# Low weight parts by accumulating DMA onto minus the high part, and small copies moved to ScalarE

## The chip, the cores and the metric

The kernel runs on one core of a Trainium2 chip. The core has five engines with a queue each: TensorE (PE in the profile; PEld is its weight load), VectorE (DVE), ScalarE (ACT), GpSimd (POOL) and SyncE (SP), which here only issues transfers. 16 DMA engines move data between DRAM and the on-chip memory (SBUF); TensorE writes to PSUM. The metric is the device time of one execution in microseconds (us): 1533.71 us, the median of three runs (1533.48 to 1533.86).

## The reference

Two layers of an encoder are applied to 640 tokens: 512 of a prompt, and 8 running streams of 16. In float32:

```python
# layer 0: mixer A|B, then ConvFFN; layer 1: attention with forget gates, then ConvFFN
def _conv_ffn(x, prev, w_up, conv_w, w_down):
    z, st = _causal_dwconv(x @ w_up, conv_w, prev)   # width 3; st: the last two rows of x @ w_up
    gate, up = jnp.split(z, 2, axis=-1)
    return (jax.nn.silu(gate) * up) @ w_down, st

hp = _rmsnorm(xp, norm_ffn[layer])                   # d_model 1024, d_ff 2816
yp, st_p = _conv_ffn(hp, zero_f, w_up[layer], conv_ffn[layer], w_down[layer])
xp = xp + yp
```

The streams start the convolution from saved rows, and `st` (two rows for each stream and for the prompt) is an output. The ConvFFN is the "channel mixer" of this text; there are two of them.

## The kernel before, in words

Activations lie with features on the 128 partitions and the 640 tokens along the free axis, in chunks of 128 features. A product in float32 accuracy is made from float32r operands: every operand is split exactly into a high part (rounded to float32r) and a low part (the rest). One chunk of one output block is then three products, high·high, high·low and low·high, each in two halves of 320 tokens: six matmuls (`mm`, line 109).

**Weights.** `weights` (line 77) forms one block of up to 128x1024 weights: SyncE loads the float32 block into `raw` (line 87), ScalarE casts it to the high part `whi` (line 88), and VectorE subtracts to give the low part `wlo` (line 89). The pool `wts` holds three buffers of each, so that the block number n+3 is formed in the buffers of block n, once TensorE has made the last product of block n.

**A channel mixer** (`ffn`, line 332). `up(j)` makes a gate block and an up block of 1024x128 weights: 48 matmuls each. `pad_evac` scales the sums by 1/rms into `zp` (lines 190 and 191) beside the saved rows, which GpSimd copies in (line 183); `new_state` copies the last two rows of each stream into the output tile `so` (line 202, GpSimd); `conv` (196, 198), SiLU (355), the product of gate and up (358, 359) and a split (97, 98) follow. The 22 pairs of blocks go in four parts of 6, 6, 5 and 5. After each part (and one `up` of the next) `project` (line 304) multiplies by the rows of the down weights that belong to it, in eight blocks of 768 or 640 columns: 36 or 30 matmuls each. The first two of the eight run side by side (the "joint" pair: all chunks but the last of both, then the last of both), so that the newest activations come last. I call the eight w0 to w7: w0 and w1 are the joint pair, w3 goes into the buffers of w0, w4 into those of w1, w5 into those of w2. In the last part of a layer each block is followed by `finish`, which in layer 0 makes the operands of the attention: `hh` and a square on ScalarE (131, 135, 138), `hl` on VectorE (132) and a running sum on GpSimd (139).

**What sets the order.** The code is written block by block; a scheduler in the build reorders it by a simulated timeline and fixes one order for each engine. At run time each engine works through its own queue in that order and waits on semaphores. GpSimd issues no DMA in this kernel; all weight loads are on SyncE's queue.

Of the kernel before, what the change touches and what calls it, by code (L numbers as in the profile page):

```python
# [8 lines left out]
F32 = mybir.dt.float32  # L9
F32R = mybir.dt.float32r  # L10
BF16 = mybir.dt.bfloat16
AF = mybir.ActivationFunctionType
ALU = mybir.AluOpType
AX = mybir.AxisListType
PSUM = bass.MemoryType.PSUM

P = 128
T = 640            # 512 prompt tokens, then 8 streams of 16
TP = 512
HT = 320           # tokens per matmul  # L20
C0 = 512 - HT      # PSUM column of token 0: the two halves meet at the bank border
NC = 8             # chunks of d_model
NB = 44            # blocks of 2*d_ff
NJ = 22
PARTS = ((0, 6), (6, 12), (12, 17), (17, 22))
ZW = 658           # 2 + 512 prompt columns, then 8 x (2 state + 16)
# [3 lines left out]
# columns of the small constants  # L30
O_CF = 0                      # ffn conv: 2 x 44 x 3
O_CB = O_CF + 2 * NB * 3      # conv_b: 4 x 3
O_ID = O_CB + 12              # identity
W_CST = O_ID + P

# columns of the constants of the first mixer
# [7 lines left out]
# columns of the constants of the attention  # L44
# [4 lines left out]
NS = 256 + 16      # keys of a stream  # L49


class Core:
    def __init__(self, ctx, tc, io):
        self.tc, self.nc, self.io = tc, tc.nc, io
        nc = self.nc
        pool = lambda es, name, **kw: es.enter_context(tc.tile_pool(name=name, reuse_waits="tile", **kw))
        self.pool = pool
        self.cp = pool(ctx, "cst", bufs=1)
        self.wp = pool(ctx, "wts", bufs=3)
        self.hp = pool(ctx, "hp", bufs=8)  # L60
        # 4 norms x 8 chunks
        self.gv = self.cp.tile([P, 32], F32, name="gv")
        nc.scalar.dma_start(out=self.gv, in_=io["gv"])
        self.cst = self.cp.tile([P, W_CST], F32, name="cst")
        self.ident = self.cst[:, O_ID:O_ID + P]
        self.ones = self.cp.tile([P, P], F32, name="ones")
        nc.gpsimd.memset(self.ones, 1.0)
        self.mhalf = self.cp.tile([P, 1], F32, name="mhalf")
        nc.scalar.mul(out=self.mhalf, in_=self.ones[:, 0:1], mul=-0.5)
        self.n = 0  # L70
# [5 lines left out]
    # ---- weights: float32 from DRAM, split exactly into two float32r parts  # L76
# [14 lines left out]

    def split(self, pool, tags, src):
        """float32 [128, 640] -> (hi, lo) float32r tiles"""
        nc = self.nc
        hi = pool.tile([P, T], F32R, tag=tags[0], name=self.nm("sh"))
        lo = pool.tile([P, T], F32R, tag=tags[1], name=self.nm("sl"))
        nc.scalar.copy(out=hi, in_=src)
        nc.vector.tensor_tensor(out=lo, in0=src, in1=hi.bitcast(F32), op=ALU.subtract)
        return hi, lo

    # ---- products, weights stationary, tokens moving
# [13 lines left out]
    def blocks(self, units, acts, order=None):  # L115
        """one output block for each unit; all share the walk over k, the last chunk closes"""
        order = list(range(len(acts))) if order is None else order
        ps = [self.psum() for _ in units]
        for part in (order[:-1], order[-1:]):
            for p_, w in zip(ps, units):  # L120
                for kc in part:
                    self.mm((p_[:, C0:512], p_[:, 512:512 + HT]), w, kc, acts[kc], kc == order[0], kc == order[-1])
        return ps

    # ---- RMS norm: operands scaled by g now, by the root later
# [28 lines left out]
    def stats(self, acc, pool, aux):  # L154
        """1/rms for each token, as columns [128, 5]"""
        nc = self.nc
        s = aux()
        for tb in range(5):
            nc.tensor.matmul(s[:, tb:tb + 1], lhsT=acc[:, tb * P:(tb + 1) * P], rhs=self.ones[:, 0:1], start=True, stop=True)
        rt = pool.tile([P, 5], F32, tag="rt", name=self.nm("rt"))  # L160
        self.rstd_of(rt, s[:, 0:5], 1.0 / 1024)
        return rt

    def spread(self, rt, pool, aux):
        """columns [128, 5] -> the same along the free axis of every partition"""
        nc = self.nc
        rb = pool.tile([P, T], F32, tag="rb", name=self.nm("rb"))
        dg = self.tmp()
        for tb in range(5):
            nc.vector.tensor_scalar(out=dg[:, tb * P:(tb + 1) * P], in0=self.ident, scalar1=rt[:, tb:tb + 1], scalar2=None, op0=ALU.mult)  # L170
        b0, b1 = aux(), aux()
        for tb in range(5):
            o = b0[:, tb * P:(tb + 1) * P] if tb < 4 else b1[:, 0:P]
            nc.tensor.matmul(o, lhsT=self.ones, rhs=dg[:, tb * P:(tb + 1) * P], start=True, stop=True)
        nc.scalar.copy(out=rb[:, 0:TP], in_=b0)
        nc.scalar.copy(out=rb[:, TP:T], in_=b1[:, 0:P])
        return rb

    # ---- causal convolution of width 3
    def pad_evac(self, zp, src, rb, states):  # L180
        """zp <- src * rb with the running streams' state before each stream"""
        nc = self.nc
        nc.gpsimd.tensor_copy(out=zp[:, 514:ZW].rearrange("p (s c) -> p s c", c=18)[:, :, 0:2],
                              in_=states.rearrange("p (s c) -> p s c", c=2))
        self.compact_mul(zp[:, 2:514], zp[:, 514:ZW].rearrange("p (s c) -> p s c", c=18)[:, :, 2:18], src, rb)

# [14 lines left out]
    def new_state(self, zp, out):  # L201
        self.nc.gpsimd.tensor_copy(out=out.rearrange("p (s c) -> p s c", c=2),  # L202
                                   in_=zp[:, 496:ZW].rearrange("p (s c) -> p s c", c=18)[:, :, 16:18])

# [6 lines left out]
    # ---- the first mixer  # L211
    def mixer_ab(self, x, load, stats, ring, finish):
        nc, io = self.nc, self.io
        rpool, rtags = ring
        with ExitStack() as es:
            mp = self.pool(es, "ab", bufs=1)
            so = mp.tile([P, 4 * 18], F32, name="sob")
            # v, tokens on partitions
# [24 lines left out]
            # the mask: a query in the first half of a chunk sees no key of the second half  # L243
# [3 lines left out]
            for tb in range(5):  # L247
                nc.scalar.activation(out=vg[:, tb, :], in_=pvs[tb], func=AF.Gelu_apprx_tanh, scale=rt[:, tb:tb + 1])
                for g in range(4):
                    j = self.tmp()  # L250
# [10 lines left out]
            for j in range(4):  # L261
                # gated causal convolution
# [19 lines left out]
            for g in range(4):  # L282
                # spatial gating
# [20 lines left out]
    def project(self, w, acts, order, x, finish, cols=1024, out=None):  # L304
        """x += w^T acts, the first two blocks side by side"""
        for obs in ((0, 1), (2,), (3,), (4,), (5,), (6,), (7,)):
            if out is not None and obs == (7,):
                self.last_block(self.weights(w[7], cols), acts, x[7], out)
                break
            ps = self.blocks([self.weights(w[ob], cols) for ob in obs], acts, order)  # L310
            for ob, p_ in zip(obs, ps):
                self.add_x(x[ob], p_)
                if finish is not None:
                    finish(ob)

    def last_block(self, w, acts, x, out):
        """the block that ends the program: one half of the tokens leaves while the other is at work"""
# [13 lines left out]
    # ---- the channel mixer  # L331
    def ffn(self, l, x, h, rb, ring, finish, out=None):
        nc, io = self.nc, self.io
        rpool, rtags = ring
        with ExitStack() as es:
# [5 lines left out]
            def up(j):  # L341
                ws = [self.weights(io["w_up"][l, b]) for b in (j, NJ + j)]
# [20 lines left out]
            for n, (a, b) in enumerate(PARTS):  # L363
# [3 lines left out]
                if n + 1 < len(PARTS):  # L367
# [3 lines left out]
                             x, finish if last else None, cols=(b - a) * P, out=out if last else None)  # L371
# [3 lines left out]
class Attention:  # L375
    """forgetting attention of 16 heads: 512 prompt tokens, and 8 streams of 16 behind 256 cached ones"""

    def __init__(self, k, es, rt, o):
# [10 lines left out]
        # sums of the streams as a product over 18 rows: the queries' sums (two parts) against ones,  # L389
        # selectors of (stream, head) against minus the keys' sums (two parts)  # L390
# [22 lines left out]
    def decay(self, h, es):  # L413
        """log forget values and their running sums, heads on partitions"""
# [12 lines left out]
        # log sigmoid(y) = min(y, 0) - log1p(e), e = exp(-|y|)  # L427
# [10 lines left out]
        # running sums, from zero at the start of each stream  # L438
# [25 lines left out]
        # minus the keys' sums, (stream, head) on partitions: cached, then new  # L464
# [12 lines left out]
        # selector rows, the same for each pair of streams  # L477
# [6 lines left out]
    def project(self, g, h, first, after_q=None):  # L484
        """q, k, v of four heads, tokens on partitions"""
# [43 lines left out]
    def operands(self, g, pair, z):  # L529
        """the four stacked operands of the two heads of a pair"""  # L530
# [32 lines left out]
    def prompt_block(self, g, pair, hh, i, z):  # L563
        """128 queries of one head"""
# [48 lines left out]
    def streams_start(self, g):  # L613
        k, nc, io = self.k, self.nc, self.io
        # the rows' own sums: [2, stream, head, token]
# [9 lines left out]
    def streams_pair(self, g, sp, z, ops):  # L625
        """the four heads of a group for two streams: rows (stream, head, token)"""
# [21 lines left out]
        # the new keys of all streams side by side, those of other streams stay at zero  # L648
# [25 lines left out]
def build(ctx, tc, io):  # L674
# [87 lines left out]
    # the output projection over the first three groups fills in behind the last one  # L762
# [36 lines left out]
def _layout(a):  # L799
# [13 lines left out]
    # small constants  # L813
# [7 lines left out]
    # first mixer  # L821
# [13 lines left out]
    # attention: cached keys [group, stream pair][head pair's features, (stream, pair, key)]  # L835
# [57 lines left out]
```

## Time and profile before

| | |
|---|---|
| median of the runs | 1533.71 us (1533.48 to 1533.86) |
| span of the profiled execution, first to last instruction | 1531.9 us |
| granted TensorE clock | 1.000 |
| TensorE busy | 1517.8 us (99%) |
| VectorE busy | 899.1 us (59%) |
| ScalarE busy | 559.4 us (37%) |
| GpSimd busy | 237.4 us (15%) |
| weight blocks formed (lines 88 and 89) | 222 |
| state copies on GpSimd (line 202) | 88 of the channel mixers, 4 of the first mixer |

The time of the profiled execution itself is the span; the median of the runs lies 1.8 us above it. The stages on the time axis, from the chain of waits and the timeline: first mixer to about 213 us, channel mixer of layer 0 to about 680, attention to about 1040, rest of its output projection to about 1060, channel mixer of layer 1 to the end. How to read a row of groups: line, engine, operation, output<-inputs, sizes and count, then busy time and the mean of one in ns, then the idle time of that engine just before these instructions with what ended it. In a timeline a row is start, duration, and in brackets the idle time before it and its releaser; SPq, ACTq and POOLq are the issuing of transfers.

### The profile page before, as it was taken

To read this page: it belongs to the slowest core of one execution; us is meant where nothing else is said; L and a number is where in the kernel's file an instruction comes from. 1 tells how busy PE (TensorE), PEld (TensorE's weight loads), DVE (VectorE), ACT (ScalarE), POOL (GpSimd) and SP (SyncE) were. 2 spreads that over 40 slices of the span, in tenths; PEclk is the share of its full clock that TensorE was granted. 3 is DMA by queue.
4 is the path that set the end of the run, shared out by engine and by line. 5 is a ranking of instruction groups with operands and counts; after the bars stand their busy time and mean duration, and the time that the engine had idled before them with its cause. 6 is when DMAs were issued, how large, how long until landed. Compare 5 with 4: busy or idle time off the path is not lost.

```text
span 1531.9 us, 26648 instructions
## 1 busy us (share of the span) xinstructions
PE 1517.8 (99%) x11008; PEld 1473.5 (96%) x11008; DVE 899.1 (59%) x1541; ACT 559.4 (37%) x918; POOL 237.4 (15%) x281
## 2 busy tenths in 40 slices
PE   8999999999999999999999999999999999999999
PEld 6999999999999999999989888888999999999998
DVE  6545437644653655675676766768765466365463
ACT  5422334322322322345545454535432233133231
POOL 5000122201210201143111111003221021021010
PEclk9999999999999999999999999999999999999999
DMA  6222212222223222243544343523222222321313
GB/s 226 77 82 73 77 56 85 68 81 85 62 64 95 64 66 93 62 156 103 180 128 136 122 123 104 183 60 107 83 60 76 87 67 57 98 73 53 107 47 106
DMA packets 52296, 142.90 MB, mean 93 GB/s; under 512 B 6656, under 2 KB 13744, under 8 KB 52048
## 3 DMA queue, kind: packets, MB, share of 16 engines
q1 hardware_dynamic: 45424, 133.79, 28.6%
q10 hardware_dynamic: 6752, 7.41, 1.4%
q8 instruction: 87, 1.43, 0.4%
q14 instruction: 33, 0.27, 0.1%
HBM read 125.41 MB, written 11.54 MB: 89 GB/s over the span
## 4 chain that ended last, share of the span: by engine, by line
PE 96%; DVE 2%; issue 1%; ACT 1%; DMA 0%; POOL 0%; SPq 0%; DVEq 0%; ACTq 0%
PE mm L109 71%; PE pj L507 10%; PE pv L583 3%; PE po L109 2%; PE pt L576 1%; PE mm L239 1%; PE pt L662 1%; PE sc L569 1%; DVE hl L132 1%; PE sc L570 1%; DVE wlo L89 1%; PE scs L641 1%; PE pt L537 1%; PE pt L655 0%; PE scs L634 0%
## 5 line engine op out<-in xcount | busy, mean ns | idle before, releaser
L88 ACT CAST whi<-raw 128x1024 fp32r<-128x1024 f32 (+4 forms) x222 | 207.6, 937 | 494.6 <-PE mm L109 426.1
L109 PE MATMUL mm<-hl,whi 128*128 128x320 f32 x1664 | 379.4, 309 | 0.5 <-DVE hl L132 0.5
L109 PE MATMUL mm<-hh,whi 128*128 128x320 f32 x1664 | 379.8, 309 | 0.0
L109 PE MATMUL mm<-hh,wlo 128*128 128x320 f32 x1664 | 379.2, 309 | 0.0
L109 PEld LDWEIGHTS mm<-hl,whi 128*128 128x128 f32 x1664 | 278.2, 188 | 0.7 <-DVE hl L132 0.7
L109 PEld LDWEIGHTS mm<-hh,whi 128*128 128x128 f32 x1664 | 278.2, 188 | 0.1
L109 PEld LDWEIGHTS mm<-hh,wlo 128*128 128x128 f32 x1664 | 278.0, 188 | 0.0
L89 DVE TENSOR_TENSOR wlo<-raw,whi 128x1024 fp32r<-128x1024 f32 (+4 forms) x222 | 245.5, 1107 | 33.3 <-ACT whi L88 33.0
L109 PE MATMUL mm<-sh,wlo 128*128 128x320 f32 x866 | 197.2, 309 | 1.3 <-DVE wlo L89 1.3
L109 PE MATMUL mm<-sl,whi 128*128 128x320 f32 x866 | 197.2, 309 | 0.0
L109 PE MATMUL mm<-sh,whi 128*128 128x320 f32 x866 | 196.2, 309 | 0.0
L202 POOL COPY so<-zp 128x18 f32<-128x18 f32 x88 | 89.4, 1016 | 570.4 <-DVE zp L191 570.4
L190 DVE TENSOR_TENSOR zp<-mm,rb 128x512 f32<-128x512 f32 x88 | 60.9, 692 | 195.8 <-PE mm L109 195.8
L209 DVE TENSOR_TENSOR x<-mm,x 128x640 f32<-128x640 f32 x79 | 65.0, 823 | 185.6 <-PE mm L109 185.6
L198 DVE SCALAR_TENSOR_TENSOR t<-zp,cst,t 128x656 f32<-128x656 f32 x184 | 165.1, 900 | 10.3 <-ACT t L196 5.6
L109 PEld LDWEIGHTS mm<-sh,wlo 128*128 128x128 f32 x866 | 144.6, 188 | 1.6 <-DVE wlo L89 1.6
L109 PEld LDWEIGHTS mm<-sl,whi 128*128 128x128 f32 x866 | 144.8, 188 | 0.0
L109 PEld LDWEIGHTS mm<-sh,whi 128*128 128x128 f32 x866 | 144.4, 188 | 0.2 <-issue 0.2
L507 PE MATMUL pj<-wlo,hh 128*128 128x256 f32 x480 | 137.7, 287 | 0.7 <-DVE wlo L89 0.7
L507 PE MATMUL pj<-whi,hh 128*128 128x256 f32 x480 | 137.7, 287 | 0.0
L507 PE MATMUL pj<-whi,hl 128*128 128x256 f32 x480 | 137.5, 287 | 0.0
L507 PEld LDWEIGHTS pj<-wlo,hh 128*128 128x128 f32 x480 | 91.6, 191 | 2.8 <-issue 1.6
(188 smaller groups left out, 1691.3 us busy)
## 6 DMA issues: line engine op xcount, KB each, us to landing
raw<-w_up SPq DMA_DIRECT2D x88, 512.0 KB
raw<-w_dn SPq DMA_DIRECT2D x32, 384.0 KB
raw<-w_c SPq DMA_DIRECT2D x24, 512.0 KB
raw<-w_dn SPq DMA_DIRECT2D x32, 320.0 KB
raw<-w_ab SPq DMA_DIRECT2D x16, 512.0 KB
ck<-c_k SPq DMA_DIRECT2D x16, 512.0 KB
cv<-c_v SPq DMA_DIRECT2D x16, 512.0 KB
o_kv<-z ACTq DMA_DIRECT2D x8, 640.0 KB
```

Of the source, the lines that this page charges most:

```text
L88: nc.scalar.copy(out=hi[:, c], in_=raw[:, c])
L89: nc.vector.tensor_tensor(out=lo[:, c], in0=raw[:, c], in1=hi[:, c].bitcast(F32), op=ALU.subtract)
L109: nc.tensor.matmul(outs[h], lhsT=l, rhs=r[:, h * HT:(h + 1) * HT], start=start and k == 0, stop=stop and k == 2)
L132: nc.vector.scalar_tensor_tensor(out=lo, in0=x, scalar=gs, in1=hi.bitcast(F32), op0=ALU.mult, op1=ALU.subtract)
L190: nc.vector.tensor_tensor(out=op, in0=a[:, 0:TP], in1=b[:, 0:TP], op=ALU.mult)
L198: nc.vector.scalar_tensor_tensor(out=cv[:, 0:CW], in0=zp[:, i:i + CW], scalar=w[:, i:i + 1], in1=cv[:, 0:CW], op0=ALU.mult, op1=ALU.add)
L202: self.nc.gpsimd.tensor_copy(out=out.rearrange("p (s c) -> p s c", c=2), in_=zp[:, 496:ZW].rearrange("p (s c) -> p s c", c=18)[:, :, 16:18])
L209: self.nc.vector.tensor_tensor(out=x, in0=ps[:, C0:C0 + T], in1=x, op=ALU.add)
L239: nc.tensor.matmul(pvs[tb], lhsT=l[:, tb * P:(tb + 1) * P], rhs=r[:, (kc % 2) * 512:(kc % 2 + 1) * 512], start=kc == 0 and k == 0, stop=kc ...
L507: nc.tensor.matmul(out[tb], lhsT=l[:, tb * P:(tb + 1) * P], rhs=r[:, c:c + 256], start=kc == 0 and i == 0, stop=kc == 7 and i == 2)
L537: nc.tensor.transpose(t[:, tb * P:(tb + 1) * P], z[i][:, tb, pair * P:(pair + 1) * P], k.ident)
L583: nc.tensor.matmul(ov[64 * hh:64 * hh + 64, i * P:n], lhsT=z[2][:, j, (2 * pair + hh) * 64:(2 * pair + hh) * 64 + 64], rhs=u[:, j * P:(j + ...
```

## The change

A second way of forming weights, `weights_added`, makes the low part without VectorE: ScalarE casts to the high part, ScalarE then writes minus the high part into the low part's tile, and a DMA that GpSimd issues reads the same float32 block from DRAM a second time and adds it onto that tile. It serves the 84 up blocks of the two channel mixers other than those of `j == 0`, and all 64 down blocks: 148 of the 222. The other 74 blocks keep the old way. `new_state` copies on ScalarE in place of GpSimd, in all 92 places. The comments are gone, which moves line numbers.

```diff
+    def weights_added(self, src, cols=1024):
+        nc = self.nc
+        raw = self.wp.tile([P, 1024], F32, tag="raw", name=self.nm("raw"))
+        hi = self.wp.tile([P, 1024], F32R, tag="whi", name=self.nm("whi"))
+        lo = self.wp.tile([P, 1024], F32R, tag="wlo", name=self.nm("wlo"))
+        nc.sync.dma_start(out=raw[:, 0:cols], in_=src)
+        nc.scalar.copy(out=hi[:, 0:cols], in_=raw[:, 0:cols])
+        nc.scalar.mul(out=lo[:, 0:cols], in_=hi[:, 0:cols].bitcast(F32), mul=-1.0)
+        nc.gpsimd.dma_start(out=lo[:, 0:cols], in_=src, accum_op=ALU.add)
+        return hi, lo
...
     def new_state(self, zp, out):
-        self.nc.gpsimd.tensor_copy(out=out.rearrange("p (s c) -> p s c", c=2),
-                                   in_=zp[:, 496:ZW].rearrange("p (s c) -> p s c", c=18)[:, :, 16:18])
+        self.nc.scalar.copy(out=out.rearrange("p (s c) -> p s c", c=2),
+                            in_=zp[:, 496:ZW].rearrange("p (s c) -> p s c", c=18)[:, :, 16:18])
...
-    def project(self, w, acts, order, x, finish, cols=1024, out=None):
+    def project(self, w, acts, order, x, finish, cols=1024, out=None, weights=None):
+        weights = weights or self.weights
...
             def up(j):
-                ws = [self.weights(io["w_up"][l, b]) for b in (j, NJ + j)]
+                ws = [(self.weights if j == 0 else self.weights_added)(io["w_up"][l, b]) for b in (j, NJ + j)]
...
                 self.project([io["w_dn"][l, ob][:, a * P:b * P] for ob in range(8)], [acts[j] for j in range(a, b)], None,
-                             x, finish if last else None, cols=(b - a) * P, out=out if last else None)
+                             x, finish if last else None, cols=(b - a) * P, out=out if last else None, weights=self.weights_added)
```

The scheduler then gives other orders at the joint pairs. Three places matter below. In the rows, the last number of a name tells tiles apart; it differs between the two kernels for the same block, and lines 88, 109, 131 and 138 before are 99 (or 88), 121, 143 and 150 in the change.

**ScalarE, end of the joint pair of the first down-projection of layer 0.** `whi_3023` before (`whi_3037` in the change) is the high part of w2, `whi_3067` (`whi_3082`) of w3, `whi_3111` (`whi_3127`) of w4. Before:

```order
L88 CAST whi_3023<-raw_3022 128x768
L196 ACTIVATE t_2923<-zp_90,cst 128x656
L97 CAST sh_2930<-t_2927 128x640
L88 CAST whi_3067<-raw_3066 128x768
L88 CAST whi_3111<-raw_3110 128x768
L88 CAST whi_3155<-raw_3154 128x768
```

In the change:

```order
L99 CAST whi_3037<-raw_3036 128x768
L100 ACTIVATE wlo_3038<-whi_3037 128x768
L214 COPY so_1994<-zp_90 128x18
L208 ACTIVATE t_2935<-zp_90,cst 128x656
L109 CAST sh_2942<-t_2939 128x640
L99 CAST whi_3082<-raw_3081 128x768
L99 CAST whi_3127<-raw_3126 128x768
L100 ACTIVATE wlo_3083<-whi_3082 128x768
L100 ACTIVATE wlo_3128<-whi_3127 128x768
L99 CAST whi_3172<-raw_3171 128x768
```

The negation for w3 (`wlo_3083`) stands behind the cast for w4. In the third part of each layer it stands directly behind its own cast; in the fourth it stands behind the cast for w4 again.

**TensorE, last part of layer 0, behind w2.** `mm_6048` before (`mm_6117`) is the sum of w2, `mm_6094` (`mm_6164`) of w3, `mm_6211` of w4 and `mm_6258` of w5. Before:

```order
L109 MATMUL mm_6048<-sh_5948,wlo_6044 128x320 x2
L109 MATMUL mm_6094<-sh_5108,whi_6089 128x320 x2
L109 MATMUL mm_6094<-sl_5109,whi_6089 128x320 x2
L109 MATMUL mm_6094<-sh_5108,wlo_6090 128x320 x2
L109 MATMUL mm_6094<-sh_5546,whi_6089 128x320 x2
```

In the change:

```order
L121 MATMUL mm_6117<-sh_6014,wlo_6112 128x320 x2
L121 MATMUL mm_6164<-sh_5158,whi_6158 128x320 x2
L121 MATMUL mm_6164<-sl_5159,whi_6158 128x320 x2
L121 MATMUL mm_6211<-sh_5158,whi_6205 128x320 x2
L121 MATMUL mm_6211<-sl_5159,whi_6205 128x320 x2
L121 MATMUL mm_6258<-sh_5158,whi_6252 128x320 x2
L121 MATMUL mm_6258<-sl_5159,whi_6252 128x320 x2
L121 MATMUL mm_6164<-sh_5158,wlo_6159 128x320 x2
```

Four matmuls each of w4 and w5 that need only high parts now stand ahead of the first one that needs the low part of w3. In layer 1 it is the same; in the first three parts of each layer only the four of w4 stand there.

**ScalarE, last part of layer 0, behind the joint pair.** `whi_6089` before (`whi_6158`) belongs to w3, `whi_6135` (`whi_6205`) to w4, `whi_6181` (`whi_6252`) to w5. Before:

```order
L88 CAST whi_6089<-raw_6088 128x640
L88 CAST whi_6135<-raw_6134 128x640
L131 ACTIVATE hh_6027<-x_74,gv 128x640
L135 ACTIVATE acc_1989<-x_74 128x640
L88 CAST whi_6181<-raw_6180 128x640
L131 ACTIVATE hh_6034<-x_75,gv 128x640
```

In the change:

```order
L99 CAST whi_6158<-raw_6157 128x640
L99 CAST whi_6205<-raw_6204 128x640
L100 ACTIVATE wlo_6159<-whi_6158 128x640
L143 ACTIVATE hh_6095<-x_74,gv 128x640
L147 ACTIVATE acc_1989<-x_74 128x640
L100 ACTIVATE wlo_6206<-whi_6205 128x640
L143 ACTIVATE hh_6102<-x_75,gv 128x640
L150 ACTIVATE t_6106<-x_75 128x640
L99 CAST whi_6252<-raw_6251 128x640
```

Eight instructions now stand ahead of the cast for w5, where there were four. In layer 1 there is no `finish` work on ScalarE, and only the two casts and the two negations stand ahead of it.

More of the change, by code (lines that the diff above doesn't have):

```diff
@@ L302, in mixer_ab @@
             self.project(io["w_oab"], y, [4, 5, 6, 7, 0, 1, 2, 3], x, finish)
-    def project(self, w, acts, order, x, finish, cols=1024, out=None):
+    def project(self, w, acts, order, x, finish, cols=1024, out=None, weights=None):
+        weights = weights or self.weights
         for obs in ((0, 1), (2,), (3,), (4,), (5,), (6,), (7,)):
             if out is not None and obs == (7,):
-                self.last_block(self.weights(w[7], cols), acts, x[7], out)
+                self.last_block(weights(w[7], cols), acts, x[7], out)
                 break
-            ps = self.blocks([self.weights(w[ob], cols) for ob in obs], acts, order)
+            ps = self.blocks([weights(w[ob], cols) for ob in obs], acts, order)
             for ob, p_ in zip(obs, ps):
```

## The prediction

> **What bounds the kernel now.** I read the chain of waits first (the work that ended last, in order of time), then the busy time of each engine by stretches. The two channel mixers are one unbroken run of matmuls each:
>
> ```profile
> 227.19 452.76 PE mm L109 x3087
> ...
> 1076.18 447.33 PE mm L109 x3050
> ```
>
> 452.76 / 3087 gives 0.1467 us for a matmul: an up block (48) takes 7.04 us, a down block of 768 columns (36) 5.28, of 640 (30) 4.40. The table by stretches (length, then busy time with count of PE, PEld, DVE, ACT, POOL, then clock, DMA share, GB/s) has these rows for an up stretch, the end of layer 0's mixer, most of layer 1's, and the end of the program:
>
> ```profile
> 240.00:310.00 70.00, 70.00 (x479) 70.00 (x478) 46.34 (x67) 25.95 (x30) 15.06 (x20) 1.00 0.23 69
> 640.00:680.00 40.00, 40.00 (x275) 40.00 (x274) 27.12 (x32) 18.84 (x26) 11.75 (x7) 1.00 0.49 158
> 1076.00:1300.00 224.00, 224.00 (x1530) 224.00 (x1529) 134.28 (x188) 77.11 (x91) 38.52 (x52) 1.00 0.25 72
> 1510.00:1532.00 22.00, 18.17 (x123) 17.64 (x121) 5.74 (x8) 1.45 (x2) 0.00 (x0) 1.00 0.23 88
> ```
>
> TensorE is busy for the whole of every stretch that the change touches except the tail, at full clock. Work taken off VectorE or GpSimd there frees engines that nobody waits for; only a new wait of TensorE can show. So the question is whether the low parts still arrive in time.
>
> **What the change removes and adds.** The groups by line and shape give the prices:
>
> ```profile
> L88 ACT CAST whi<-raw 128x1024 fp32r<-128x1024 f32 x140 | 146.7, 1049 | 325.7 <-PE mm L109 264.9 <-issue 39.6 <-PE aux L239 10.7
> L88 ACT CAST whi<-raw 128x768 fp32r<-128x768 f32 x37 | 30.9, 836 | 94.3 <-PE mm L109 91.9 <-PE po L109 1.3 <-ACT p L591 1.0
> L88 ACT CAST whi<-raw 128x640 fp32r<-128x640 f32 x32 | 23.1, 728 | 68.6 <-PE mm L109 66.3 <-issue 1.4 <-ACT t L138 0.9
> L89 DVE TENSOR_TENSOR wlo<-raw,whi 128x1024 fp32r<-128x1024 f32 x140 | 173.3, 1240 | 28.6 <-ACT whi L88 28.3
> L202 POOL COPY so<-zp 128x18 f32<-128x18 f32 x88 | 89.4, 1016 | 570.4 <-DVE zp L191 570.4
> L251 ACT ACTIVATE t<-vg 128x128 f32<-128x128 f32 x20 | 5.9, 305 | 0.0
> ```
>
> VectorE loses 148 subtractions (1.24 us for 1024 columns), GpSimd its 92 state copies (1.02 us). Both lay beside full TensorE work: gain nothing. ScalarE gains 148 negations, priced as casts of the same shape (1.05, 0.84, 0.73 us: 84, 32 and 32 of them, 138 us), and 92 copies, bounded by the 0.31 us of a 128x128 activation above and nothing below. In the 224 us stretch ScalarE was busy for 77, so it has room; what matters is what stands in its queue ahead of a cast. The state copies wait for the same `zp` as the convolution behind them, and cost the path nothing.
>
> **The accumulating transfer** is in no trace. The nearest row is a plain load of 256 KB on SyncE's queue at the very start, issued at 0.74 and consumed at 3.43:
>
> ```profile
> 0.74 0.38 SPq L87 DMA_DIRECT2D raw<-w_v  x1
> ...
> 3.43 0.62 ACT L88 CAST whi<-raw 128x512 fp32r<-128x512 f32 x1 [0.76 <-DMA raw<-w_v]
> ```
>
> That is 2.69 us. The up stretch above moves 69 GB/s at a share of 0.23, so 300 GB/s with all DMA engines busy: 0.87 us for 256 KB, 1.8 us fixed. From below, priced as a plain load: 3.1 us for 384 KB, 2.9 for 320, 3.55 for 512. An add must also read what lies in the tile, so I take twice the bytes (2.6, 2.2 and 3.5 us), 1.0 us for the issue on GpSimd (its nearest small instruction is the 1.02 us copy), and at the down blocks 0.8 us because the two casts there also release two plain loads of 1.3 us each onto the same engines: **6.2 us for 384 KB, 5.8 for 320, 6.3 for 512**. From above, three times the bytes: 7.5, 7.1 and 8.05. Beyond that the engines themselves are the bound: 1.75 us (the plain load of an up block) plus three times 1.75 fills the 7.04 us of its matmuls. A gain is excluded, since TensorE is full. [...]
>
> **Where it hides.** In the steady case block n+3 starts two blocks after block n ends, and needs its low part four matmuls later (0.59 us): 14.7 us for an up block, of which cast and negation take 2.2. 12.5 us are left for 6.3. For later down blocks 9.4 and 7.8 us are left for 6.2 and 5.8. Hidden; this cover is gone only beyond 12.5 us.
>
> **Where it does not.** w3 uses the buffers of w0, which come free almost at the end of the joint pair, and only w2 lies between. ScalarE before, at the first, third and last joint pair of layer 0:
>
> ```profile
> 323.33 1.71 ACT L88 CAST whi<-raw 128x768 fp32r<-128x768 f32 x2 [3.97 <-PE mm L109]
> 329.49 0.84 ACT L88 CAST whi<-raw 128x768 fp32r<-128x768 f32 x1 [4.45 <-PE mm L109]
> ...
> 560.93 0.73 ACT L88 CAST whi<-raw 128x640 fp32r<-128x640 f32 x1 [2.20 <-PE mm L109]
> ...
> 566.21 0.73 ACT L88 CAST whi<-raw 128x640 fp32r<-128x640 f32 x1 [3.67 <-PE mm L109]
> ...
> 654.94 1.36 ACT L88 CAST whi<-raw 128x640 fp32r<-128x640 f32 x2 [4.70 <-PE mm L109]
> 656.21 0.82 ACT L131 ACTIVATE hh<-x,gv 128x640 fp32r<-128x640 f32 x1
> 656.94 0.72 ACT L135 ACTIVATE acc<-x 128x640 f32<-128x640 f32 x1
> 657.73 0.73 ACT L88 CAST whi<-raw 128x640 fp32r<-128x640 f32 x1
> ```
>
> (a) First two parts, both layers. The casts for w3 and w4 end at 325.04, the negation for w3 (now behind both) at 325.88. w2 ends 0.09 before the next cast, at 329.40; eight matmuls on high parts follow (1.17 us), so the low part is needed at 330.57. 4.7 us against 6.2: 1.5 us lost, four times: **6.0** (0 to 11.2).
>
> (b) Third part: cast and negation are neighbours, done at 560.93 + 1.46 = 562.4; needed at 566.1 + 1.17 = 567.3. 4.9 against 5.8: 0.9, twice: **1.8** (0 to 4.4).
>
> (c) Last part of layer 0. The negation ends at 656.30 + 0.73 = 657.03, the transfer at 662.8. w0 is free at 654.85; 17 matmuls later w2 ends (657.34), 12 more on high parts would end at 659.1: **3.7** lost. There is a floor: four of the twelve need the high part of w5, whose cast began at 657.73 and now has two negations, one more `hh` and one more square ahead of it (0.73 + 0.73 + 0.73 + 0.72 by their spacing): it ends near 661.4, where eight matmuls are done at 658.5. 2.9 us go even if the transfer costs nothing; 5.0 at the upper price.
>
> (d) Last part of layer 1, without that `finish` work: **3.7** (0.8 to 5.0).
>
> (e) The fourth up block of layer 0, whose buffers come free at the end of the first, joint pair of up blocks:
>
> ```profile
> 227.00 0.59 ACT L175 COPY rb<-aux 128x512 f32<-128x512 f32 x1 [11.56 <-PE aux L174]
> 227.48 0.27 ACT L176 COPY rb<-aux 128x128 f32<-128x128 f32 x1
> 228.29 2.00 ACT L88 CAST whi<-raw 128x1024 fp32r<-128x1024 f32 x2 [0.54 <-ACT rb L176]
> ```
>
> In the change the two `rb` copies stand between its cast and its negation: 228.29 + 1.05 + 0.86 + 1.05 = 231.25. The joint pair ends near 229.2, the low part is needed 7.04 + 0.59 later: 5.55 against 6.3: **0.75** (0 to 2.5). In layer 1 the window is a microsecond longer, and nothing is lost (1.5 at the upper price).
>
> **The sum** is 6.0 + 1.8 + 3.7 + 3.7 + 0.75 = 16 us (3.7 to 29.6). 1531.9 + 16 = 1547.9 for the span, and with the 1.8 us by which the median of the runs lies above it, **1550 us**.
>
> **The rivals.**
>
> *A quick transfer* (not slower, or hardly). If the add costs no more than a plain load, (a), (b) and (e) vanish, and 2.9 + 0.8 remain: 1537.4. For it: 300 GB/s is far from used at a share of 0.23. Against: a second read per element. If in addition the order in (c) costs less than I read, it is no change at all. That decides below about 4.7 us for 384 KB.
>
> *A slow add.* If the DMA engines need over three times the bytes' time for it, they become the bound of both mixers. At 3.5 times, an up block needs 1.75 + 6.1 = 7.9 us instead of 7.04 (84 blocks: 71 us), the down blocks in proportion (37): about 1640. For it: nothing here shows the rate of an add. Against: it would have to be more than the second read explains.
>
> *Faster.* VectorE no longer subtracts, so sums leave PSUM earlier. But TensorE waits for no VectorE work in the stretches above; the tail has 3.8 us of idle time that hangs on the last add and store, which are not touched. At most 1 us; over 3 us I have no place for.
>
> *The change doesn't do what it says*, and the low parts still come from VectorE: the subtractions are gone from VectorE's queue in the order, so no chance for it.
>
> **How the numbers follow.** Forecast (stalls at joint pairs, 1538 to 1565) 0.57; quick transfer 0.17, of which 0.08 within 0.2% of before; no change at all 0.05; slow add 0.18; faster 0.03. 0.2% is 3.1 us, about what a measurement of this kernel can tell from none. So faster 0.03, same 0.13, slower 0.84. The range goes from 1535 (part of the quick transfer) to 1620 (most of what lies between the upper price and the slow add); the forecast's own range is 1537.4 to 1563.
>
> **What would show it.** TensorE's idle time should be in ten places, ended by a DMA into `wlo`: behind w2 of each part, and at the fourth up block, with none in steady up blocks. In (c) the cast of w5 should end it or come within a microsecond of doing so. The DMA share in up stretches should rise from 0.23 to about 0.7. I am wrong if `wlo` waits appear in every block (slow add), if TensorE stays unbroken (quick), or if a wait appears behind GpSimd's queue, where the row copies of line 183 and the running sums of `finish` now stand among the transfers.

## The result and the profile after

The changed kernel takes 1558.03 us (median; 1556.94 to 1562.75) against 1533.78 us before: 1.0162 times as long, 95% interval 1.0146 to 1.0178, or 24.3 us. The profiled execution has a span of 1561.0 us, 29.1 more than before, at a mean granted clock of 0.993; the other three have spans of 1555.2 to 1557.0 at 0.995 to 0.997.

Whom TensorE waited for in the changed kernel (total, times, longest):

```profile
PE mm L121 <- DMA wlo<-w_dn: 13.0, 8, 4.5
PE mm L251 <- ACT hh L143: 5.5, 1, 5.5
PE mm L251 <- DVE wlo L89: 2.5, 1, 2.5
PE mm L121 <- DMA wlo<-w_up: 2.3, 3, 1.6
PE mm L121 <- ACT whi L99: 2.1, 1, 2.1
```

In the kernel before, the two longest rows for low parts from VectorE were these (its line 239 is 251 here):

```profile
PE mm L239 <- DVE wlo L89: 1.6, 1, 1.6
PE mm L109 <- DVE wlo L89: 1.3, 1, 1.3
```

The rows with `wlo<-w_dn`, `wlo<-w_up` and `whi` are new, 17.35 us in twelve waits. TensorE's timeline places them; these are the ones of over a microsecond (in brackets the wait and what ended it):

```profile
240.73 0.56 PE L121 MATMUL mm<-hh,wlo 128*128 128x320 f32 x2 [1.63 <-DMA wlo<-w_up]
336.06 0.56 PE L121 MATMUL mm<-sh,wlo 128*128 128x320 f32 x2 [1.20 <-DMA wlo<-w_dn]
...
575.36 0.56 PE L121 MATMUL mm<-sh,wlo 128*128 128x320 f32 x2 [1.78 <-DMA wlo<-w_dn]
670.91 0.57 PE L121 MATMUL mm<-sh,whi 128*128 128x320 f32 x2 [2.06 <-ACT whi L99]
673.83 0.90 PE L121 MATMUL mm<-sh,wlo 128*128 128x320 f32 x2 [2.06 <-DMA wlo<-w_dn]
...
1324.82 0.56 PE L121 MATMUL mm<-sh,wlo 128*128 128x320 f32 x2 [1.25 <-DMA wlo<-w_dn]
1436.87 0.55 PE L121 MATMUL mm<-sh,wlo 128*128 128x320 f32 x2 [1.79 <-DMA wlo<-w_dn]
...
1534.29 0.90 PE L121 MATMUL mm<-sh,wlo 128*128 128x320 f32 x2 [4.46 <-DMA wlo<-w_dn]
```

They stand behind w2 of each part and at the fourth up block. The four left out are short: w3 in the second part of layer 0 (0.28) and the first of layer 1 (0.16), the fourth up block of layer 1 (0.43), an up block late in layer 1 (0.25). The other up blocks have none, as a stretch of layer 0 and one of layer 1 in the changed kernel show (columns as in the prediction):

```profile
242.00:300.00 58.00, 58.00 (x398) 58.00 (x397) 28.43 (x45) 29.53 (x40) 10.37 (x17) 1.00 0.69 143
1104.00:1180.00 76.00, 76.00 (x521) 76.00 (x520) 37.59 (x58) 38.14 (x53) 13.89 (x22) 1.00 0.68 140
```

The DMA share went from 0.23 to 0.69 at twice the GB/s. The page's parts on queues and on issues (the last number is the median from issue to landing in us) give the price of the transfers:

```profile
q1 hardware_dynamic: 45424, 133.79, 27.3%
q0 software_dynamic: 21312, 67.12, 26.8%
```
```profile
wlo<-w_up POOLq DMA_DIRECT2D x84, 512.0 KB, 6.2
wlo<-w_dn POOLq DMA_DIRECT2D x32, 384.0 KB, 5.7
wlo<-w_dn POOLq DMA_DIRECT2D x32, 320.0 KB, 5.6
```

The added queue (q0) took nearly the time of SyncE's (q1) for half its bytes.

17.35 us of waiting are not 29.1. TensorE's busy time rose too, from 1517.8 to 1528.6 us, though its work is the same. Two things make that up. **Refilling**, as I call it (what TensorE does in that time no run shows): the pairs of matmuls behind a wait start 0.26 us later than the wait alone explains. These are the pairs of matmuls ahead of and behind the wait at 240.73:

```profile
238.65 0.46 PE L121 MATMUL mm<-hl,whi 128*128 128x320 f32 x2
...
241.12 0.46 PE L121 MATMUL mm<-hh,whi 128*128 128x320 f32 x2
```

The next pair would have started at 238.94; it starts 1.79 us later, and the pair behind it (241.12) another 0.1 late, 1.89 us for a wait of 1.63. The waits of 1.20 and 1.79 us at 336.06 and 1436.87 cost 1.46 and 2.05 in the same way. At 0.26 us each, an estimate from these three, the twelve waits cost 3.1 us beside themselves. **Half clock**: cut into pieces of 3.41 us around three of the waits, the table by stretches reads (granted clock third from the end):

```profile
572.79:576.20 3.41, 1.63 (x11) 1.36 (x10) 0.48 (x1) 0.82 (x2) 0.86 (x1) 1.00 1.07 239
576.20:579.61 3.41, 3.41 (x15) 3.41 (x14) 0.00 (x0) 0.00 (x0) 0.00 (x0) 0.50 0.73 183
1432.92:1436.33 3.41, 2.17 (x15) 1.90 (x13) 0.82 (x1) 1.47 (x2) 0.86 (x1) 1.00 1.05 215
1436.33:1439.74 3.41, 2.87 (x19) 2.87 (x20) 0.00 (x0) 0.00 (x0) 0.00 (x0) 1.00 1.04 274
1528.49:1531.90 3.41, 1.34 (x9) 1.01 (x7) 0.38 (x1) 0.75 (x2) 1.67 (x2) 1.00 1.06 348
1531.90:1535.31 3.41, 1.02 (x4) 1.02 (x5) 0.00 (x0) 0.00 (x0) 0.00 (x0) 0.50 1.09 254
1535.31:1538.72 3.41, 3.41 (x14) 3.41 (x14) 0.00 (x0) 0.00 (x0) 0.00 (x0) 0.50 0.41 78
1538.72:1542.13 3.41, 3.41 (x25) 3.41 (x25) 0.82 (x1) 1.47 (x2) 0.22 (x1) 1.00 0.01 5
```

In the piece behind the wait at 575.36 TensorE makes 15 matmuls where 25 are usual. Its pairs start 0.53 us apart there, where 0.29 is usual:

```profile
577.00 0.74 PE L121 MATMUL mm<-sh,whi 128*128 128x320 f32 x2
577.53 0.74 PE L121 MATMUL mm<-sl,whi 128*128 128x320 f32 x2
```

So about 45% of TensorE's busy time at half clock is lost. This execution has four such stretches, from 19.8, 576.2, 671.8 and 1531.9 us, 3.4, 3.4, 6.8 and 6.8 us long. TensorE is busy for 16.06 us of them, a loss of 7.2 us. The first lies outside the change, behind a wait at the program's start that varied from 1.1 to 2.5 us between the profiles of this study; up to there all the kernels have the same matmuls in the same order. The sum: 17.35 waiting, 0.86 more waiting at the start (2.49 for 1.63), 3.1 refilling and 7.2 half clock are 28.5, against 29.1 measured; 0.6 us are not placed.

### The profile page after: what moved, and what is told of

It is laid out like the page before. It is cut to its first block, busy times and chain, and to the rows that moved or that the text cites. A ratio compares the mean times of both kernels' runs of the same rounds, so it can differ in the third digit from the quotient of the medians.

```text
span 1561.0 us, 26870 instructions
## 1 busy us (share of the span) xinstructions
PE 1528.6 (98%) x11008; PEld 1480.0 (95%) x11008; DVE 751.7 (48%) x1393; ACT 696.4 (45%) x1158; POOL 272.6 (17%) x337
## 3 DMA queue, kind: packets, MB, share of 16 engines
q0 software_dynamic: 21312, 67.12, 26.8%
## 4 chain that ended last, share of the span: by engine, by line
PE 85%; DMA 5%; issue 5%; DVE 2%; ACT 1%; POOL 1%; SPq 0%; POOLq 0%; DVEq 0%; ACTq 0%
PE mm L121 62%; PE pj L520 10%; DMA wlo<-w_dn 4%; PE pv L596 3%; PE po L121 2%; DMA wlo<-w_up 1%; PE pt L589 1%; PE mm L251 1%; PE pt L675 1%; PE sc L582 1%; DVE wlo L89 1%; DVE hl L144 1%; PE sc L583 1%; PE scs L654 1%; PE pt L550 1%
## 5 line engine op out<-in xcount | busy, mean ns | idle before, releaser
L99 ACT CAST whi<-raw 128x1024 fp32r<-128x1024 f32 (+2 forms) x148 | 137.9, 933 | 310.3 <-PE mm L121 305.7
L121 PEld LDWEIGHTS mm<-sh,wlo 128*128 128x128 f32 x866 | 146.2, 190 | 17.0 <-DMA wlo<-w_dn 15.4
L100 ACT ACTIVATE wlo<-whi 128x1024 fp32r<-128x1024 f32 (+2 forms) x148 | 139.1, 943 | 4.1
L101 POOL DMA_DIRECT2D wlo<-w_up x84 | 72.9, 868 | 355.9 <-ACT so L214 257.1
L88 ACT CAST whi<-raw 128x1024 fp32r<-128x1024 f32 (+3 forms) x74 | 69.5, 942 | 125.2 <-PE mm L121 68.5
```

The source lines that it names most:

```text
L88: nc.scalar.copy(out=hi[:, c], in_=raw[:, c])
L99: nc.scalar.copy(out=hi[:, 0:cols], in_=raw[:, 0:cols])
L100: nc.scalar.mul(out=lo[:, 0:cols], in_=hi[:, 0:cols].bitcast(F32), mul=-1.0)
L101: nc.gpsimd.dma_start(out=lo[:, 0:cols], in_=src, accum_op=ALU.add)
L121: nc.tensor.matmul(outs[h], lhsT=l, rhs=r[:, h * HT:(h + 1) * HT], start=start and k == 0, stop=stop and k == 2)
```

## The experiments

**1. The state copies alone.** The kernel before with the second part of the change.

```diff
-        self.nc.gpsimd.tensor_copy(out=out.rearrange(...), in_=zp[...])
+        self.nc.scalar.copy(out=out.rearrange(...), in_=zp[...])
```

> Only the second part of the change: the kernel before with the last rows of the convolution copied by ScalarE. Theory (all of the loss is the late low parts): no change, 1533.7 us within 1 us, granted clock 1.00, no wait of TensorE for ScalarE in the channel mixers. Rival (the copies delay ScalarE's casts and take part in the loss): 1536 us or more, with waits for casts of high parts.

1534.95 us against 1534.21, ratio 1.0005 (0.9996 to 1.0014). No wait for ScalarE in the channel mixers. The time is 1.2 us above the 1533.7 that was expected, but 0.7 above the kernel before in its own session. The copies cost nothing that can be told.

**2. The old way for the 28 blocks with the least time, and 3. its complement.**

```diff
# 2
-    ws = [(self.weights if j == 0 else self.weights_added)(...) for b in (j, NJ + j)]
+    ws = [(self.weights if j <= 1 else self.weights_added)(...) for b in (j, NJ + j)]
-    ps = self.blocks([weights(w[ob], cols) for ob in obs], acts, order)
+    ps = self.blocks([(self.weights if ob in (3, 4, 5) else weights)(w[ob], cols) for ob in obs], acts, order)
# 3: the same two lines with the two ways exchanged (j != 1; weights for 3, 4, 5, self.weights for the others)
```

> The change, but w3, w4 and w5 of every part of the down-projection (24 blocks) and the two up blocks of j = 1 in each layer (4) form their low part with VectorE again; 120 of the 148 accumulating transfers stay. Theory (the loss sits at the joint pairs and the fourth up block, and the lower clock follows from the waits there): at most 0.3 us of waiting for low parts is left (the late up block near the end of layer 1), granted clock 1.00, 1534 to 1536 us. Rival (the transfers slow TensorE or its clock everywhere by their load): most of the 24 us stays, 1548 us or more, clock below 1.00.

> The complement: accumulating transfers for w3, w4 and w5 of every part and the two up blocks of j = 1 alone (28 transfers); the other 120 blocks form their low part with VectorE. Theory: nearly the same waits as with all 148, somewhat shorter since the plain loads and fewer transfers share the engines: 14 to 17 us of waiting, 1550 to 1558 us, clock 0.995 to 0.998. Rival (load of the transfers): a fifth of the loss, about 1539 us.

Number 2, with 120 of the 148 transfers, takes 1534.31 us, ratio 1.0001 (0.9992 to 1.0010). Both mixers in its table by stretches, with TensorE's only idle time that of the tail:

```profile
220.00:680.00 460.00, 460.00 (x3143) 460.00 (x3143) 203.28 (x302) 209.88 (x285) 81.93 (x107) 1.00 0.64 142
1076.00:1532.00 456.00, 452.31 (x3083) 451.79 (x3082) 191.82 (x288) 196.83 (x268) 69.32 (x100) 1.00 0.64 138
```

The DMA engines are nearly as busy as in the change (0.64 for 0.68 and 0.69), and TensorE's clock and matmuls don't notice. Number 3, with 28 transfers, takes 1554.74 us, ratio 1.0133 (1.0118 to 1.0149): 20.5 of the 24 us. Its waits are shorter than expected, 11.9 us where 14 to 17 were, and the fourth up blocks have none. So the loss is not the load of the transfers but the 28 places, and this was tested from both sides.

**4. The waits filled with work.**

```diff
         for k, (l, r) in enumerate(((wh, ah), (wh, al), (wl, ah))):
+            if k == 2 and fill:
+                d = self.aux()
+                for i in range(fill):
+                    nc.tensor.matmul(d[:, 0:HT], lhsT=wh, rhs=ah[:, 0:HT], start=i == 0, stop=i == fill - 1)
# fill on the first chunk only: w3 of parts 3 and 4 with 10 and 28, the fourth up block of layer 0 with 8
```

> The change, with extra matmuls of 128x320 whose sums nobody reads, put ahead of the first low product of w3: 10 in the third part of each layer (1.5 us), 28 in the last (4.1 us), and 8 in the fourth up block of layer 0 (1.2 us). They take the place of waiting, so the low parts arrive when they did. Theory (the lower clock comes from TensorE's idle time): clock 1.00 in both channel mixers, TensorE idle there for under 6 us, and the time falls by the half-clock share although work was added: 1552 to 1554 us. Rival (the lower clock comes from something else, the transfers' load or the matmuls on new weights): clock 0.993 to 0.997 as in the change, 1557 us or more.

1558.27 us, ratio 1.0153 (1.0139 to 1.0167), the time of the change; the expected 1552 to 1554 was missed, and by the time alone the rival holds. But the composition is another, and the clock is the theory's. Its profile has a span of 1556.5, and one stretch of half clock in the mixers where the change had three:

```profile
PE mm L125 <- DMA wlo<-w_dn: 5.8, 8, 1.8
...
PE mm L125 <- DMA wlo<-w_up: 1.5, 3, 0.8
```

7.24 us of waiting are left, 10.1 less, and 84 extra matmuls add 12.3. The half clock's loss fell by 5.7 us, from 7.2 to 1.5, and the wait at the start by 0.8: 12.3 - 10.1 - 5.7 - 0.8 = -4.3, against -4.5 between the two spans. The clocks of its runs are 0.998 to 1.000, where the change's are 0.993 to 0.997, with all 148 transfers in place. In these runs the half clock followed TensorE's idle time. What I got wrong is the waiting left over (I had less than 6 us in mind, and forgot to count the refilling): w3 in the last part of layer 0 still waited 1.82 us, and the one half-clock stretch follows it.

**5. Four buffers.**

```diff
-        hi = self.wp.tile([P, 1024], F32R, tag="whi", name=self.nm("whi"))
-        lo = self.wp.tile([P, 1024], F32R, tag="wlo", name=self.nm("wlo"))
+        hi = self.wp.tile([P, 1024], F32R, tag="whi", name=self.nm("whi"), bufs=4)
+        lo = self.wp.tile([P, 1024], F32R, tag="wlo", name=self.nm("wlo"), bufs=4)
```

> The change with four buffers for the high and low parts in place of three, so that w3 no longer waits for the buffers of w0 (w4 does, with a block more between). Theory (the waits come from buffers that come free late): no wait of TensorE for a low part, clock 1.00, 1533 to 1535.5 us with all 148 transfers in place. Rival (the transfers themselves are too slow or load the core): 1545 us or more.

1538.60 us, ratio 1.0019 (1.0010 to 1.0028). With a buffer of its own w3 has no wait; 1.8 of 17.35 us are left, both in last parts. The time missed the expected range by 3 us: its profile has two half-clock stretches outside the mixers, behind 2.2 us of waiting at the start and at the end of the attention (1043.5 us). Why the attention got them with four buffers is open.

**6. A plain transfer in place of the adding one.** It leaves the addition out, so the low parts are the whole weights.

```diff
-        nc.gpsimd.dma_start(out=lo[:, 0:cols], in_=src, accum_op=ALU.add)
+        nc.gpsimd.dma_start(out=lo[:, 0:cols], in_=src.bitcast(F32R))
```

> The change with the same transfer from GpSimd as a plain copy: the addition is left out, so the low part's tile holds the whole weight. It has the same issue, bytes and place in the chain, without the read of what lies there. Theory (the add costs the bytes twice): lands 1.2 to 1.3 us sooner for 384 and 320 KB, its queue's time per byte halves, waits for low parts fall from 15.3 to 6 to 8 us, 1543 to 1548 us. Rival (the fixed part of a GpSimd transfer is nearly all of it): waits as in the change, 1555 us or more.

1545.96 us, ratio 1.0073 (1.0059 to 1.0086), as expected. Its queue and its issues:

```profile
q0 software_dynamic: 21312, 67.12, 15.4%
```
```profile
wlo<-w_up POOLq DMA_DIRECT2D x84, 512.0 KB, 4.6
wlo<-w_dn POOLq DMA_DIRECT2D x32, 384.0 KB, 4.0
wlo<-w_dn POOLq DMA_DIRECT2D x32, 320.0 KB, 3.9
```

15.4% of 1543.7 us against 26.8% of 1561.0 for the same bytes: the add takes 1.76 times the engines' time of a copy, and lands 1.6 to 1.7 us later. Of these 0.33 are the issue on GpSimd (0.86 us with the add, 0.53 without), which leaves the 1.2 to 1.3 expected for the bytes. Of the waits 6.3 us are left, all in the last parts: 2.06 for the cast of w5 and 0.50 for w3 in layer 0, 3.71 for w3 in layer 1, where its plain transfer took 5.95 us rather than 3.9.

**7. Two halves.**

```diff
-        nc.gpsimd.dma_start(out=lo[:, 0:cols], in_=src, accum_op=ALU.add)
+        n = cols // 2
+        for c in (slice(0, n), slice(n, cols)):
+            nc.gpsimd.dma_start(out=lo[:, c], in_=src[:, c], accum_op=ALU.add)
```

> The change with each accumulating transfer cut into two of half the columns, the half that TensorE needs first issued first. Theory (half of the latency is the engines' time for the bytes): the first half lands 1.3 us sooner, the waits in parts 1 and 2 and at the fourth up block vanish, 0.5 us each are left in part 3 and about 3 us in the last parts: 1542 to 1548 us. Rival (fixed latency): waits as in the change, 1555 us or more; or the second half, issued 0.9 us later, is now late: waits in the middle of w3.

1549.21 us, ratio 1.0093 (1.0079 to 1.0106), a microsecond above the range. The first halves landed 4.4, 4.2 and 4.4 us after their issue (medians for the blocks of 512, 384 and 320 KB), 1.8, 1.5 and 1.2 sooner than the whole, where 1.3 was expected; the second halves, issued 0.54 us behind them, took 5.7, 4.8 and 4.9. So half the bytes are worth 1.2 to 1.8 us, and an estimate of 2.6 to 3.2 us of the latency does not shrink with them. Waits of 8.75 us are left: none at the fourth up block and in three of the four first parts, but 1.40 in the other, and 7.35 of them in the last parts and part 3. The 1.40 are for w4, whose first half was issued 2.5 us behind its negation (the second half of w3 went out ahead of it, at 1311.30) and took 7.9.

**8. Negation on VectorE.**

```diff
-        nc.scalar.mul(out=lo[:, 0:cols], in_=hi[:, 0:cols].bitcast(F32), mul=-1.0)
+        nc.vector.tensor_scalar(out=lo[:, 0:cols], in0=hi[:, 0:cols].bitcast(F32), scalar1=-1.0, scalar2=None, op0=ALU.mult)
```

> The change with the negation on VectorE in place of ScalarE. Theory: in the last part of layer 0 the cast of w5 is no longer behind two negations, so the wait for ScalarE (2.06 us) goes, but TensorE then waits as long for the low part of w3, since its transfer starts at about the same time (within 0.3 us): the sum of the two waits stays 3.5 to 4.2 us, and the time 1555 to 1559 us. Rival (ScalarE's order is the floor and the transfer hides behind it): the last part of layer 0 loses 2 us less, 1553 us or less.

1555.30 us, ratio 1.0133 (1.0118 to 1.0149). The last part of layer 0:

```profile
663.41 0.56 PE L121 MATMUL mm<-sh,whi 128*128 128x320 f32 x2 [0.66 <-ACT whi L99]
667.05 0.56 PE L121 MATMUL mm<-sh,wlo 128*128 128x320 f32 x2 [2.80 <-DMA wlo<-w_dn]
```

0.66 + 2.80 in place of 2.06 + 2.06: the order on ScalarE costs 0.7 us of 4.1 at most (the second profile of the change, experiment 11, has 3.8 in this place), and behind it the transfer sets the end, as expected. Not expected was that the waits in the mixers fell to 13.0 us in all, with 1.1 in place of 3.6 in the third parts; why is open.

**9. Only w4 and w5 the old way**, w3 left as in the change.

```diff
-            ps = self.blocks([weights(w[ob], cols) for ob in obs], acts, order)
+            ps = self.blocks([(self.weights if ob in (4, 5) else weights)(w[ob], cols) for ob in obs], acts, order)
```

> The change with w4 and w5 of every part formed by VectorE again (16 blocks); w3 and the other 131 keep the accumulating transfer. TensorE's order then has 18 matmuls of w4 in parts 1 and 2 (9 in part 3, 45 of w4 and w5 in the last) between the first four of w3 and its first low product, where the change has 4 (8 in the last). Theory (a late low part costs only what TensorE has no other work for): w3's transfer still takes 4 to 6 us, but nothing waits for it in parts 1, 2 and 4, at most 1 us in part 3; the fourth up block keeps its 1.6 us: 1535 to 1538 us. Rival (w3's transfer itself is the cost): 1545 us or more.

1542.44 us, ratio 1.0044 (1.0027 to 1.0060), above the expected 1535 to 1538. w3 itself hardly waits now (0.34 us in the last part of layer 0): other work stands before its low part. But w3 ends later for it, and so do its buffers come free later. In the last part of layer 0 its 26 last matmuls run from 670.60 to 674.4, and the block that takes the buffers over follows:

```profile
674.42 0.73 ACT L99 CAST whi<-raw 128x640 fp32r<-128x640 f32 x1 [5.08 <-PE mm L121]
```
```profile
683.50 0.57 PE L121 MATMUL mm<-sh,wlo 128*128 128x320 f32 x2 [1.63 <-DMA wlo<-w_dn]
```

Four waits for down blocks (3.2 us) remain, this one the longest, beside 1.6 for the fourth up block and 0.7 for two others. The wait had moved on from w3 to a later block. Of the profile's own excess of 10.0 us over before, 5.5 are waiting, 1.8 refilling, and 2.4 the start (a wait 0.86 longer and 1.5 of half clock).

**10. The kernel before with four buffers**, the candidate for a version that beats both.

> The kernel before, no accumulating transfer, with four buffers for the high and low parts. It is the candidate for a version faster than both. Theory: three waits of TensorE for VectorE's low parts outside the channel mixers (1.6, 1.3 and 0.7 us in the trace of before) shrink: 1531.5 to 1534 us. Rival (those waits are set by loads or by VectorE and not by buffers): no change within 1 us.

1536.02 us, ratio 1.0011 (1.0002 to 1.0021): not faster, and above the expected 1531.5 to 1534. Of the three waits that were to shrink the 1.3 and the 0.7 us are gone, but the one at the start is 1.93, and others grew (the one for `hl` behind the attention from 0.46 to 1.08). No version tried beats the kernel before.

**11. The changed kernel once more.**

> The changed kernel a second time, for what differs between executions. Theory: the waits of TensorE stay within 1 us of the first trace at each place (17.4 us in all in the channel mixers), while the stretches at half clock can fall elsewhere: after the waits of 2 us and more in the last parts for certain, after those of 1.6 to 1.8 us by chance. Rival (the half clock belongs to fixed places): the same four stretches.

Span 1563.1 us, 17.53 us of waits in the mixers. The places are the same but for the late up block, which has no wait; the lengths differ by up to 1.3 us (second part of layer 0: 1.62 for 0.28; third of layer 1: 0.76 for 1.79). Half clock began at 19.3, 241.1, 579.1, 674.6 and 1534.8 us. Two pairs of pieces of it:

```profile
237.70:241.10 3.40, 1.61 (x11) 1.35 (x10) 2.31 (x5) 2.99 (x5) 0.06 (x1) 1.00 1.06 236
241.10:244.51 3.41, 3.41 (x15) 3.41 (x14) 1.80 (x2) 1.23 (x2) 1.00 (x2) 0.51 0.97 238
463.00:466.40 3.40, 1.78 (x12) 1.52 (x11) 0.83 (x1) 1.68 (x2) 0.86 (x1) 1.00 1.01 194
466.40:469.81 3.41, 3.41 (x25) 3.41 (x24) 0.00 (x0) 0.00 (x0) 0.00 (x0) 1.00 0.90 201
```

The wait at the fourth up block, 1.78 us here and 1.63 in the first trace, now brought the half clock; 1.62 us at 466 did not.

## Why the prediction was right, and what it missed

Forecast were 1550 us (range 1535 to 1620) and stalls at the joint pairs; measured 1558.03, the stalls where they were put. Step by step, in us of waiting:

| step | predicted | first profile | second profile |
|---|---|---|---|
| (a) parts 1 and 2, both layers | 6.0 | 2.9 | 4.5 |
| (b) part 3 | 1.8 | 3.6 | 2.8 |
| (c) last part, layer 0 | 3.7 | 4.1 | 3.8 |
| (d) last part, layer 1 | 3.7 | 4.5 | 4.1 |
| (e) fourth up block | 0.75 | 2.1 | 2.3 |
| a late up block | 0 | 0.25 | 0 |
| sum | 16 | 17.35 | 17.5 |

**The price of the transfer** held: 6.2, 5.8 and 6.3 us were put from the end of the negation for 384, 320 and 512 KB, of which 1.0 for the issue. Medians of 5.7, 5.6 and 6.2 from the issue, plus 0.3 between negation and issue, are 6.0, 5.9 and 6.5. Every transfer that ended a wait was issued 0.29 to 0.31 us behind its negation, so nothing waited behind GpSimd's queue. Its central assumption, twice the bytes for an add, was my estimate, which no trace of before showed; experiment 6 measured 1.76 times the engines' time of a copy. The share of 0.69 in up stretches was called about 0.7. **Hidden elsewhere** held (experiment 2).

**The single terms** are off by what the one price could not hold: landing varies from 4.4 to 9.0 us in the first profile. In (a) w3's transfer took 4.95 to 6.04 us, in (b) 6.7 where the median for 320 KB is 5.6. In (d) three adds, two loads and three stores of outputs go out within 4 us (1526.0 to 1529.6); the chain of waits has

```profile
1527.54 6.70 DMA wlo<-w_dn
```

and the DMA share is 1.06 and 1.09 in the two rows from 1528.49. Only two plain loads had been charged beside an add. In (e) the 512 KB took 8.5 us in layer 0 and 7.3 in layer 1 against the median of 6.2, which is why layer 1's fourth up block, priced at nothing, lost 0.4 to 0.5 too; what slowed them there is open. That the sum of the waits still came within 1.4 us is in part luck: (a) was 3.1 us too high, all the others together 4.5 too low. The upper price for 320 KB is 6.9 us by its own terms (1.8 + 3.3 + 1.0 + 0.8) and not 7.1, so the upper end of the sum is 28.8; nothing hangs on it. **The floor in (c)** was there at 2.06 instead of 2.9 us, and the transfer ended behind it, as the sum had it.

**The step that failed** is the last one, the sum itself: it took a microsecond of waiting for a microsecond of time. The missing terms are refilling, 3.1 us, and the half clock, 5.7 us in the mixers of the profiled execution. 17.35 and 3.1 are 20.5 of the median's 24.3; what remains is about the half clock's, which is smaller in the timed executions (0.995 to 0.997) than in the profiled one. The rows of before had shown the granted clock at 1.00 throughout, and a wait of 1.63 us at its start without consequence; I had no row for a longer one, and the sum put nothing for it.

**The rivals.** The quick transfer was put at 1537.4. Experiment 6 made the transfer quick and got 1546: (a), (b) and (e) vanished as said, but (d) kept 3.71 us for the 0.8 put, since the plain transfer, too, was slow in the burst there (5.95 us, at a DMA share of 1.06), and the half clock followed. The slow add (1640) would have needed 3 times the bytes' time; it has 1.76. No gain came from VectorE, though its busy time fell from 899.1 to 751.7 us.

## What the runs showed of the hardware

In these profiles the half clock fell on a grid. In each of the six with more than one stretch of it, all of them begin at the same phase of a period of 3.413 us, to 0.1 us (in the first one at 19.82, 576.19, 671.77 and 1531.92: 95.58 us are 28 periods, 1512.10 are 443), and last one or two periods; the phase differs between executions (2.76 us there, 2.22 in the second profile of the change). In nine profiles (two of the change, and experiments 3 to 9) I summed TensorE's waits in each period, from 8 us on at the start, in both mixers and in the output projection ahead of the second. All 20 periods with 52% or more of waiting, entered at full clock, were followed by half clock; of 27 with 30 to 51%, none. (A twenty-first stretch, in the attention of experiment 5, followed 44% of listed waits, in a stretch of many short gaps.) So 1.63 us of waiting cost its own time and the refilling, 1.78 us cost 1.5 more where they fell into one period, 1.79 us nothing more where they fell into two (1436.87), and 3.26 us, split in two by the grid, cost nothing more in experiment 7. Once at half clock a period with 20 to 30% of waiting kept it there (experiments 3, 6, 7, 8 and 11).

## What to carry to other kernels

Price a change that adds latency at the block whose buffers come free last, with everything that is issued there at once; the average block says nothing: 120 of 148 transfers were free, 28 cost 20 us. Then price the wait as more than its length: here 0.26 us of refilling each and, from about 1.8 us within one period of 3.413 us on, half-clock stretches of 3.4 or 6.8 us, in which some 45% of TensorE's busy time was lost. Other work put before a late operand helped here only as far as the buffers behind it could come free later: in experiment 9 w3's wait fell to 0.34 us, and the block that takes its buffers over waited 1.63.
